# Expert weights in halves: 8 KB tiles for gate and up, and a new place for each weight transfer's issue

## The chip, the core and the metric

The kernel runs on one core of a Trainium2 chip. The metric is the device time of one execution in microseconds. The core has five engines that run side by side: PE (TensorE, matrix products), ACT (ScalarE), DVE (VectorE), POOL (GpSimd) and SP (SyncE, which here only issues DMA transfers). Sixteen DMA engines move data between HBM and the on-chip memory.

## What is computed

Two layers of a decoder over 1024 tokens of width 1024, all in float32. Each layer is a mixer (two groups of eight attention heads) followed by a mixture of experts, with a final norm behind the second layer. The change lies in the experts. Each token picks one of 8 groups and 2 of the 4 experts in it; each of the 32 experts has three matrices:

```python
def expert_block(args):
    xb, e = args
    h = jax.nn.silu(xb @ w_gate[e]) * (xb @ w_up[e])   # w_gate, w_up: 1024 x 256
    return h @ w_down[e]                               # w_down: 256 x 1024
...
contrib = ybuf[dest].astype(jnp.float32) * g_sorted[:, None]
y = jax.ops.segment_sum(contrib, tok_sorted, num_segments=T)
```

## The kernel before

A float32 product is made of three passes on TensorE (`mm3`, L190): each operand is split into a rounded part "hi" and a remainder "lo", and hi x hi, hi x lo and lo x hi are added up. So every weight that arrives must first be cast: ACT writes hi (L1464), DVE writes lo (L1465).

One layer runs as mixer, output projection with routing (loop at L1245), then the experts. The experts' loop (L1556) has 33 turns. In turn n TensorE makes the gate and up products of expert n in two halves (`gate_up`, 8 chunks of 128 rows of the weights), the transposes of expert n+1's tokens (`turn_x`) and the down products of expert n-1 (`down`, 2 chunks). Each expert has one block of 96 token rows, gathered by POOL three turns ahead; POOL also scatters the results.

The casts go in pieces of 128 x 1024 numbers, six for an expert: pieces 0 to 3 are its gate and up weights (two chunks of both matrices each), pieces 4 and 5 its down weights. `ORDER` (L52) fixes their sequence: in turn n come (n,4), (n,5), (n+1,0), (n+1,1), (n+1,2), (n+1,3). Seven pairs of hi and lo tiles (NHL, L46) go round among them.

The order of work on PE, ACT, DVE and POOL is written out by hand (`manual_schedule`, L96). SP is not in that list: a planner places its transfers, with the order in which they are written as their priority, and waits for a tile's room to be free.

Raw weights arrive as follows. Gate and up of one expert share one tile of 16 KB a partition (`gu_tile`, L333): two transfers of 1 MB (`load_gu`, L336), each partition reading 8 rows of 256 numbers, 8 KB in one run. The pool "mix" (L842) holds four such tiles; in the mixer the same four hold `mixT`, the transposed mixer output (hi and lo). Expert 0 has a tile of its own (L1234). Experts 1 to 3 are loaded in the routing loop (L1293), expert 4 when the experts' stage is opened (L1526), and expert n+5 by `load_a`, written at the head of turn n (L1558); its room is that of expert n+1. The down weights have four tiles of 8 KB a partition (`load_dn`, L330: one transfer of 1 MB, 8 KB runs); `load_b` of expert e+4 is written behind piece (e,5) (L1548). In the last layer tiles of the same pool take the residual for the final norm (L1583).

The hidden values of an expert (`hs`) are transposed in two parts (`flip_h`, L1493), with the column order that the layout of the down weights asks for.

Of the kernel before, what the change touches and what calls it, by code (L numbers as in the profile page):

```python
# [9 lines left out]
F32 = mybir.dt.float32  # L10
# [10 lines left out]
P = 128  # L21
# [60 lines left out]
def kernel(ctx: ExitStack, tc: tile.TileContext, x, positions, attn_norm, w_in, b_f, q_norm, w_uq,  # L82
# [245 lines left out]
        return [gain_flip] + [w[0][0], w[1][0], w[0][1], w[2][0], w[1][1], w[3][0], w[2][1], w[3][1]]  # L328

    def load_dn(raw, wd_, eng):  # L330
        eng.dma_start(raw, wd_.rearrange("(p k) n -> p k n", k=2))

    def gu_tile(p, tag="mix"):  # L333
        return p.tile([P, 2, KC, FF], F32, name="gu", tag=tag)

    def load_gu(raw, wg_, wu_):  # L336

        for g, w_ in enumerate((wg_, wu_)):
            sp.dma_start(raw[:, g], w_.rearrange("(p k) n -> p k n", k=KC))

    def wa_load(raws, l, k):
        raw = raws.tile([P, 512], F32, name="raw")[:, :MISC]
# [23 lines left out]
    def mixer(l, opened):  # L366
# [472 lines left out]
        pp_close()  # L839


        mp, mp_close = open_pool(f"mix{l}", "right", 4)  # L842
        mixT = [mp.tile([P, 2, KC, 2 * P], F32R, name="mix") for _ in range(4)]
        wor, wor_close = open_pool(f"wor{l}", "right", 2)
        att, att_close = open_pool(f"att{l}", "left", 3)
        tps, tps_close = open_pool(f"tps{l}", bufs=2, space=PSUM)
# [101 lines left out]
        def fin_c(p, half, bank=1):  # L948
            ysb = pairs[p][0].rearrange("p t s d -> p t (s d)")

            pt = ybank[bank].rearrange("p (t n) -> p t n", n=P)
            for i in range(4):
                pe.transpose(pt[:, i], ysb[:, half * 4 + i], ident)
            g = gain("fox" if p < 4 else "mla", l, p % 4)
            ms = [([mixT[2 * half + q][:, s] for s in range(2)], pt[:, 2 * q:2 * q + 2].rearrange("p a b -> p (a b)")) for q in range(2)]
            for m, src in ms:
                act.activation(m[0][:, p], src, AF.Copy, scale=g)
            for m, src in ms:
                dve.scalar_tensor_tensor(m[1][:, p], src, g, m[0][:, p].bitcast(F32), op0=OP.mult, op1=OP.subtract)
# [27 lines left out]
        ht_ = {}  # L987

        def out_mm(i, c, ks):
            m, ts, cs = [mixT[i // 2][:, s] for s in range(2)], slice(i % 2 * P, (i % 2 + 1) * P), slice(c * 512, c * 512 + 512)  # L990
            if ks[0] == 0:
                ht_[i, c] = ybank[0] if (i, c) == (1, 1) else op_.tile([P, 512], F32, name="ps")
            mm3(ht_[i, c], lambda k: m[0][:, k, ts], lambda k: m[1][:, k, ts],
                lambda k: w_at(k, 0, cs), lambda k: w_at(k, 1, cs), ks, first=ks[0] == 0, last=ks[-1] == KC - 1)
# [108 lines left out]

        def halves(j):
            hi, lo = hl[j]
            raw = early[0][:, :, 2 * j:2 * j + 2].rearrange("p g k n -> p g (k n)")
            hi, lo = (w.rearrange("p (g n) -> p g n", g=2) for w in (hi, lo))
            act.activation(hi, raw, AF.Copy)
            pool.tensor_tensor(lo, raw, hi.bitcast(F32), op=OP.subtract)
# [121 lines left out]

        hts = {i: resid(i) for i in range(2)}

        early = [v1.tile([P, 2, KC, FF], F32, name="V", tag="V")]  # L1234
        load_gu(early[0], w_gate[l, 0], w_up[l, 0])
        groups, going, state = {4: (0, 4), 6: (4, 6)}, deque(), [None]

        def route_on(n, pe_=False):
# [6 lines left out]
        for i in range(NT):  # L1245
            if i + 2 < NT:
                hts[i + 2] = resid(i + 2)
            if i > 1:
                out_mm(i, 0, range(4))
                if i < 4:  # L1250
                    route_b(i - 2)
                if i > 2:
                    route_a(i - 1, 0)
                    route_a(i - 1, 1)
                out_mm(i, 0, range(4, KC))
            add(i, 0)
            if i == NT - 1:
                norm_half(0)
            route_on(ROA)
            if i:  # L1260
                out_mm(i, 1, range(4))
                route_on(1, True)
                if i > 2:
                    route_b(i - 1)
                else:
                    route_a(i - 1, 0)
                    route_a(i - 1, 1)
                if i == NT - 1:
                    route_a(i, 0)
                out_mm(i, 1, range(4, KC))  # L1270
            if i == NT - 1:

                ops_close()
                vr2_close()
                hp, hl_close = open_pool(f"hl{l}")
                hl = slots(hp, 4)
                halves(0)
            add(i, 1)
            if i in groups:
                going.append(route_group(fs, *groups[i]))  # L1280
            if i < NT - 1:
                route_on(ROB)
                norm(i)
            else:
                route_a(i, 1)
                route_on(ROB)
                norm_half(1)
                route_b(i)
                halves(1)
                norm(i)  # L1290
                halves(2)
                halves(3)
            if i % 2 and i < NT - 1:  # L1293
                early.append(gu_tile(mp))
                load_gu(early[-1], w_gate[l, len(early) - 1], w_up[l, len(early) - 1])
            if i in DNAT:
                j = DNAT.index(i)
                load_dn(downs[j], w_down[l, j], sp)
# [102 lines left out]
    def slots(p, n):  # L1401
        return [[p.tile([P, D], F32R, name=f"{w}{i}") for w in ("hi", "lo")] for i in range(n)]

    def moe_open(l, v0, v1, mp, early, downs, dn_close, hl, hl_close, spare_close):
        scatters, parts = [], {}

        def pools_for(n, deep):
            rw, c1 = open_pool(f"er{n}{l}", "right")
            if deep:
                downs.extend(rw.tile([P, 2, D], F32, name=f"dn{j}") for j in range(2, NDN))  # L1410
            hp, c2 = open_pool(f"eh{n}{l}", "right")
            pools = {"rw": rw, "hl": deque(hl + slots(hp, NHL - 4) if deep else slots(hp, 6)), "gu": (mp, "mix") if deep else (rw, "gu0")}

            def more():
                pools["xs"], c3 = open_pool(f"ex{n}{l}", "left", 2 if deep else 1)
                pools["pp"], c4 = open_pool(f"ep{n}{l}", bufs=2, space=PSUM)
                pools["close"] = lambda: (c4(), c3(), c2(), c1(), (dn_close(), hl_close()) if deep else None)

            return pools, more

        def expert(pools, wg_, wu_, wd_, gi, si, n=None):
# [4 lines left out]
            ps_ = lambda *a, **k: pools["pp"].tile(*a, **k)  # L1426
            par = 0 if n is None else n % 2

            def load_a():
                if n is not None and n < len(early):  # L1430
                    raw = early[n]
                else:
                    raw = gu_tile(*gp)
                    load_gu(raw, wg_, wu_)
                e["raw"] = [raw[:, :, 2 * j:2 * j + 2].rearrange("p g k n -> p g (k n)") for j in range(4)]

            def parts_of(pairs):
                for hi, lo in pairs:
# [54 lines left out]
            def flip_h():  # L1493
                pt = ps_([P, 4, RB], F32, name="ph", bufs=1)
                for c in range(2):
                    pe.transpose(pt[:, c], e["hs"].rearrange("r (p k) -> r k p", k=2)[:, c], ident[0:RB, 0:RB])
                e["hT"] = [parts["xt"][:, 2 * par + s, KC * RB:(KC + 2) * RB].rearrange("p (k r) -> p k r", r=RB) for s in range(2)]
                split(e["hT"][0], e["hT"][1], pt[:, 0:2])

# [38 lines left out]
    def moe(l, m):  # L1538
# [5 lines left out]
        def pieces_to(n):  # L1544
            while pieces and n_pieces - len(pieces) < n:
                e, j = pieces.popleft()
                E[e]["piece"](j, pool if j in ONPOOL else dve)
                if j == 5 and e + NDN < NE:  # L1548
                    E[e + NDN]["load_b"]()

        pieces_to(PC0)
        E[0]["turn_x"]()
# [2 lines left out]
        kept = []  # L1555
        for n in range(NE + 1):  # L1556
            cur, prev, nxt = (E[k] if 0 <= k < NE else None for k in (n, n - 1, n + 1))
            if n + 5 < NE:  # L1558
                E[n + 5]["load_a"]()
            if n + NXB < NE:  # L1560
                E[n + NXB]["gather"]()
            if cur:
                cur["gate_up"](0)
            pieces_to(6 * n + PC[0])
            if prev:
                prev["flip_h"]()
            if cur:
                cur["gate_up"](1)
            if nxt:
                nxt["turn_x"]()  # L1570
            if prev:
                prev["down"]()
            pieces_to(6 * n + PC[1])
            if cur:
                cur["silu"]()
            if nxt:
                nxt["split_x"]()
            pieces_to(6 * n + PC[2])
            if prev:
                prev["result"]()  # L1580
            if l == DEPTH - 1 and n >= KEPT and len(kept) < NT:

                raw = gu_tile(mp).rearrange("p g k n -> p (g k n)")  # L1583
                for t in range(4):
                    kept.append(raw[:, t * D:(t + 1) * D])
                    sp.dma_start(kept[-1], h_d[2 * l][len(kept) - 1])
            pieces_to(6 * n + 6)
        pools["close"]()
        if l < DEPTH - 1:
# [101 lines left out]
```

## Time and profile before

| | us |
|---|---|
| median of 3 runs | 1969.77 (1967.16 to 1974.84) |
| the profiled execution, device time | 1971.02 |
| its span, first to last instruction | 1969.2 |
| TensorE busy | 1753.9 (89%) |
| VectorE busy | 1360.1 (69%) |
| ScalarE busy | 1178.5 (60%) |
| GpSimd busy | 651.4 (33%) |

The durations come from the one profiled execution. An engine's busy share is an average over the mixer, the routing and the experts, which have different limits, so the stages are looked at one by one. In the slices of the page each digit stands for 49 us; a 9 means 90% or more. In a timeline row the first number is the start, the second the duration (of all instructions merged into the row, "x3"), and the bracket tells how long the engine sat idle before it and what ended that. "SPq" rows are issues: the time is that of issuing, not of moving the data.

### The profile page before, as it was taken

Reading aid. Unit: us, or ns where it says so; the run is one execution under the profiler, and the core shown is the slowest. Engines: PE = TensorE matmul, PEld = TensorE weight load, DVE = VectorE, ACT = ScalarE, POOL = GpSimd, SP = SyncE. Lnnn points to the kernel's source line nnn. Section 1 sums busy time; section 2 is a strip of 40 time slices with the busy share of each in tenths; the row PEclk is TensorE's granted clock in tenths of the full one; section 3 lists DMA queues with packets and bytes.
Section 4 is the critical chain, followed back from the end, with each engine's and each line's share of the span. In section 5 each row is a group of like instructions: output and inputs, shape, how many; then the busy total and the mean of one; then the engine's idle time right before and its main releaser. Section 6 shows DMA issues by size and latency. Waiting matters only on the chain. (4 is left out here: it accounts for less than half of the span.)

```text
span 1969.2 us, 33380 instructions
## 1 busy us (share of the span) xinstructions
PE 1753.9 (89%) x12509; PEld 1414.7 (72%) x12509; DVE 1360.1 (69%) x2172; ACT 1178.5 (60%) x2254; POOL 651.4 (33%) x857
## 2 busy tenths in 40 slices
PE   7999799999994999999499997999999769999970
PEld 6987688888883776666399876888878647766640
DVE  6464389887346898888665345888853679987865
ACT  4443378888213888777344235888851258877751
POOL 4001154234105334554330021623341333345525
PEclk9999999999996999999799998999999979999985
DMA  4247832453754899998841775344446469999966
GB/s 159 65 120 219 269 125 102 107 128 80 276 176 147 314 364 373 363 363 292 289 147 52 205 232 201 122 109 109 109 172 227 171 218 359 366 368 357 362 238 219
DMA packets 118753, 427.07 MB, mean 217 GB/s; under 512 B 20118, under 2 KB 35516, under 8 KB 90940
## 3 DMA queue, kind: packets, MB, share of 16 engines
q1 hardware_dynamic: 103676, 387.13, 58.7%
q0 software_dynamic: 14336, 33.58, 5.1%
q10 hardware_dynamic: 576, 4.19, 0.7%
q8 instruction: 100, 1.64, 0.4%
q14 instruction: 65, 0.53, 0.1%
HBM read 347.24 MB, written 94.37 MB: 224 GB/s over the span
## 5 line engine op out<-in xcount | busy, mean ns | idle before, releaser
L1465 DVE TENSOR_TENSOR lo<-gu,hi 128x1024 fp32r<-128x1024 f32 x248 | 294.0, 1218 | 12.3 <-ACT hi L1464 11.5
L1464 ACT ACTIVATE hi<-gu 128x1024 fp32r<-128x1024 f32 x248 | 255.4, 1059 | 0.0
L1514 POOL DMA_INDIRECT y<-V,sidx x64 | 139.2, 2175 | 328.8 <-ACT V L1513 314.2
L873 PE MATMUL S<-op 96*128 96x512 f32 (+3 forms) x960 | 229.0, 372 | 19.5 <-DMA op<-FK 12.7
L885 DVE TENSOR_REDUCE nm<-S 128x1 f32<-128x1024 f32 (+7 forms) x256 | 183.2, 752 | 68.9 <-PE S L877 68.8
L894 ACT ACTIVATE pr<-S,nm 128x1024 f32<-128x1024 f32 (+7 forms) x256 | 189.2, 755 | 37.6 <-DVE nm L885 37.5
L195 PE MATMUL gu<-lo,V 128*96 128x512 f32 x512 | 205.2, 401 | 6.9 <-DVE lo L1465 6.7
L194 PE MATMUL gu<-hi,V 128*96 128x512 f32 x512 | 206.9, 404 | 0.5 <-ACT V L184 0.5
L196 PE MATMUL gu<-hi,V 128*96 128x512 f32 x512 | 205.6, 402 | 1.0
L1465 DVE TENSOR_TENSOR lo<-dn,hi 128x1024 fp32r<-128x1024 f32 x128 | 156.4, 1223 | 62.6 <-ACT hi L1464 59.1
L904 ACT ACTIVATE ph<-pt 128x512 f16<-128x512 f32 x288 | 157.3, 601 | 66.9 <-PE pt L902 65.9
L905 DVE SCALAR_TENSOR_TENSOR pl<-pt,ph 128x512 f16<-128x512 f32 x288 | 184.7, 683 | 8.7 <-ACT ph L904 7.8
L873 PEld LDWEIGHTS S<-op 96*128 96x128 f32 (+1 forms) x960 | 161.5, 196 | 36.9 <-DMA wor<-in_w_o_dram 14.9
L1464 ACT ACTIVATE hi<-dn 128x1024 fp32r<-128x1024 f32 x128 | 135.0, 1056 | 75.4 <-DMA dn<-in_w_down_dram 75.4
L902 PE MATMUL pt<-ident,pr 128*128 128x128 f32 x1152 | 154.9, 278 | 8.6 <-DVE pl L905 3.6
L902 PEld LDWEIGHTS pt<-ident,pr 128*128 128x128 f32 x1152 | 125.2, 143 | 14.0 <-ACT pr L894 13.2
L916 PE MATMUL y<-V,ph 128*128 128x64 f16 x2304 | 121.6, 193 | 2.8 <-ACT ph L904 1.6
L195 PEld LDWEIGHTS gu<-lo,V 128*96 128x96 f32 x512 | 83.5, 163 | 52.4 <-DVE lo L1465 22.7
L916 PEld LDWEIGHTS <-ph 128*128 128x128 f16 x2304 | 116.9, 98 | 5.2 <-ACT ph L904 1.8
L916 PE MATMUL y<-V,pl 128*128 128x64 f16 x1152 | 117.0, 193 | 1.1 <-DVE pl L905 1.0
L196 PEld LDWEIGHTS gu<-hi,V 128*96 128x96 f32 x512 | 83.1, 162 | 46.2 <-DVE V L185 14.8
L175 POOL TENSOR_SCALAR rs_v<-ss 128x1 f32<-128x1 f32 (+1 forms) x44 | 20.3, 461 | 289.3 <-ACT xn L1096 151.0
(363 smaller groups left out, 4393.7 us busy)
## 6 DMA issues: line engine op xcount, KB each, us to landing
gu<-in_w_gate_dram SPq DMA_DIRECT2D x62, 1024.0 KB
gu<-in_w_up_dram SPq DMA_DIRECT2D x62, 1024.0 KB
dn<-in_w_down_dram SPq DMA_DIRECT2D x60, 1024.0 KB
raw<-in_w_in_dram SPq DMA_DIRECT2D x48, 256.0 KB
h<-ht SPq DMA_DIRECT2D x17, 512.0 KB
FQ<-st SPq DMA_DIRECT2D x32, 256.0 KB
FK<-st SPq DMA_DIRECT2D x32, 256.0 KB
MQ<-st SPq DMA_DIRECT2D x16, 512.0 KB
```

The source lines that it names most:

```text
L194: pe.matmul(ps, sh(kc), mh(kc), start=first and i == 0, stop=False)
L195: pe.matmul(ps, sh(kc), ml(kc), start=False, stop=False)
L196: pe.matmul(ps, sl(kc), mh(kc), start=False, stop=last and i == n - 1)
L873: pe.matmul(o, a[0:k, qs], b[0:k, c0:c0 + n], start=bank not in started, stop=pi == len(passes) - 1 and not diag, skip_group_check=True)
L885: dve.tensor_reduce(nm, u["S"][:, col:col + (qb + 1) * P], axis=AX.X, op=OP.max, negate=True)
L894: act.activation(u["pr"][:, s], u["S"][:, s], AF.Exp, bias=nm, accum_out=zst[h // 2][:, qb, h % 2:h % 2 + 1])
L902: pe.transpose(pt[:, b], u["pr"][:, (4 * q + b) * P:(4 * q + b + 1) * P], ident)
L904: act.activation(u["ph"][:, ks], pt, AF.Copy, scale=P_SCALE)
L905: dve.scalar_tensor_tensor(u["pl"][:, ks], pt, P_SCALE, u["ph"][:, ks], op0=OP.mult, op1=OP.subtract)
L916: pe.matmul(yst[h][:, qb], a[:, b], v[:, kb, h % H, c], start=first_y[h], stop=(kb == qb and s == 2), skip_group_check=True)
L1464: act.activation(h_, raw, AF.Copy)
L1465: eng.tensor_tensor(l_, raw, h_.bitcast(F32), op=OP.subtract)
```

## The change

Gate and up of an expert are loaded in two halves. A half (`gu_half`) is a tile of 8 KB a partition that holds four of the eight rows of both matrices in every partition: two transfers of 512 KB, in runs of 4 KB. The pool "mix" has eight tiles of this size instead of four of twice the size, and `mixT` takes them as separate tiles for hi and lo. Expert 0's own tile is laid out by halves as well, with four transfers.

The transfers of experts 5 to 31 are written elsewhere: the first half of expert e+4 behind piece (e,1), the second behind piece (e,3), where `load_b` already stands behind piece (e,5). The line at the head of the turn is gone.

The down weights are laid out with chunk c holding rows 128c to 128c+127 (before: every second row), so that a partition reads two runs of 4 KB; `flip_h` takes contiguous columns accordingly. The tiles of the last residual loads are halved in size. Only what follows from the layouts is left out below.

```diff
     def load_dn(raw, wd_, eng):
-        eng.dma_start(raw, wd_.rearrange("(p k) n -> p k n", k=2))
-
-    def gu_tile(p, tag="mix"):
-        return p.tile([P, 2, KC, FF], F32, name="gu", tag=tag)
-
-    def load_gu(raw, wg_, wu_):
-
+        eng.dma_start(raw, wd_.rearrange("(k p) n -> p k n", p=P))
+
+    def gu_half(p, wg_, wu_, q, tag="mix"):
+
+        raw = p.tile([P, 2, KC // 2, FF], F32, name="gu", tag=tag)
+        ks = slice(q * 4, q * 4 + 4)
         for g, w_ in enumerate((wg_, wu_)):
-            sp.dma_start(raw[:, g], w_.rearrange("(p k) n -> p k n", k=KC))
+            sp.dma_start(raw[:, g], w_.rearrange("(p k) n -> p k n", k=KC)[:, ks])
+        return raw
...
-        mp, mp_close = open_pool(f"mix{l}", "right", 4)
-        mixT = [mp.tile([P, 2, KC, 2 * P], F32R, name="mix") for _ in range(4)]
+        mp, mp_close = open_pool(f"mix{l}", "right", 8)
+        mixT = [[mp.tile([P, KC, 2 * P], F32R, name="mix") for _ in range(2)] for _ in range(4)]
...
-        early = [v1.tile([P, 2, KC, FF], F32, name="V", tag="V")]
-        load_gu(early[0], w_gate[l, 0], w_up[l, 0])
+        raw0 = v1.tile([P, 2, 2, 4, FF], F32, name="V", tag="V")
+        early = [[raw0[:, 0], raw0[:, 1]]]
+        for q in range(2):
+            for g, w_ in enumerate((w_gate, w_up)):
+                sp.dma_start(raw0[:, q, g], w_[l, 0].rearrange("(p k) n -> p k n", k=KC)[:, q * 4:q * 4 + 4])
...
             if i % 2 and i < NT - 1:
-                early.append(gu_tile(mp))
-                load_gu(early[-1], w_gate[l, len(early) - 1], w_up[l, len(early) - 1])
+                early.append([gu_half(mp, w_gate[l, len(early)], w_up[l, len(early)], q) for q in range(2)])
...
-            def load_a():
+            def load_a(*qs):
                 if n is not None and n < len(early):
-                    raw = early[n]
+                    raw = e["halves"] = early[n]
                 else:
-                    raw = gu_tile(*gp)
-                    load_gu(raw, wg_, wu_)
-                e["raw"] = [raw[:, :, 2 * j:2 * j + 2].rearrange("p g k n -> p g (k n)") for j in range(4)]
+                    raw = e.setdefault("halves", [])
+                    for q in qs or range(2):
+                        raw.append(gu_half(gp[0], wg_, wu_, q, gp[1][q]))
+                if len(raw) < 2:
+                    return
+                e["raw"] = [raw[q][:, :, k:k + 2].rearrange("p g k n -> p g (k n)") for q in range(2) for k in (0, 2)]
...
-                    pe.transpose(pt[:, c], e["hs"].rearrange("r (p k) -> r k p", k=2)[:, c], ident[0:RB, 0:RB])
+                    pe.transpose(pt[:, c], e["hs"][:, c * P:(c + 1) * P], ident[0:RB, 0:RB])
...
                 if j == 5 and e + NDN < NE:
                     E[e + NDN]["load_b"]()
+                if j in (1, 3) and 0 < e < NE - 4:
+                    E[e + 4]["load_a"](j // 2)
...
-            if n + 5 < NE:
-                E[n + 5]["load_a"]()
...
-                raw = gu_tile(mp).rearrange("p g k n -> p (g k n)")
-                for t in range(4):
-                    kept.append(raw[:, t * D:(t + 1) * D])
-                    sp.dma_start(kept[-1], h_d[2 * l][len(kept) - 1])
+                for raw in [mp.tile([P, 2, 4, FF], F32, name="gu", tag="mix") for _ in range(2)]:
+                    for t in range(2):
+                        kept.append(raw[:, t].rearrange("p k n -> p (k n)"))
+                        sp.dma_start(kept[-1], h_d[2 * l][len(kept) - 1])
```

## Rows read from the trace of the kernel before

**Rows 1.** The page: busy us, share and instructions; DMA share in 40 slices.

```profile
PE 1753.9 (89%) x12509; PEld 1414.7 (72%) x12509; DVE 1360.1 (69%) x2172; ACT 1178.5 (60%) x2254; POOL 651.4 (33%) x857
...
DMA  4247832453754899998841775344446469999966
```

**Rows 2.** Windows of layer 0's experts: length, busy by engine, clock, DMA share, GB/s.

```profile
660.00:757.00 97.00, 97.00 (x488) 70.60 (x487) 91.09 (x107) 86.39 (x128) 36.60 (x31) 1.00 1.01 365
757.00:905.00 148.00, 143.24 (x680) 95.83 (x679) 121.99 (x145) 116.28 (x176) 77.40 (x45) 1.00 0.98 364
914.00:930.00 16.00, 15.09 (x68) 9.89 (x69) 14.62 (x20) 13.84 (x22) 4.02 (x2) 1.00 0.54 210
```

**Rows 3.** Timeline of ACT, casts of layer 0: start, us, instruction, idle before.

```profile
758.66 1.06 ACT L1464 ACTIVATE hi<-dn 128x1024 fp32r<-128x1024 f32 x1 [1.23 <-DMA dn<-in_w_down_dram]
...
860.59 1.06 ACT L1464 ACTIVATE hi<-dn 128x1024 fp32r<-128x1024 f32 x1 [2.42 <-DMA dn<-in_w_down_dram]
...
930.91 1.06 ACT L1464 ACTIVATE hi<-dn 128x1024 fp32r<-128x1024 f32 x1 [1.27 <-DMA dn<-in_w_down_dram]
...
934.99 2.01 ACT L1464 ACTIVATE hi<-gu 128x1024 fp32r<-128x1024 f32 x2
...
938.79 1.07 ACT L1464 ACTIVATE hi<-dn 128x1024 fp32r<-128x1024 f32 x1
```

**Rows 4.** Waits (us in total, times, longest), 820 to 880, then 900 to 960.

```profile
ACT hi L1464 <- DMA dn<-in_w_down_dram: 12.1, 6, 2.6
...
ACT wah L184 <- DMA y<-V,sidx: 5.4, 1, 5.4
```

**Rows 5.** Timeline of SP, weight transfers issued in layer 0.

```profile
639.60 0.34 SPq L331 DMA_DIRECT2D dn<-in_w_down_dram  x1
649.11 0.33 SPq L339 DMA_DIRECT2D gu<-in_w_gate_dram  x1
...
694.35 0.33 SPq L339 DMA_DIRECT2D gu<-in_w_gate_dram  x1
...
695.20 0.42 SPq L331 DMA_DIRECT2D dn<-in_w_down_dram  x1
...
749.53 0.33 SPq L339 DMA_DIRECT2D gu<-in_w_gate_dram  x1
...
832.81 0.33 SPq L331 DMA_DIRECT2D dn<-in_w_down_dram  x1
...
860.58 0.33 SPq L339 DMA_DIRECT2D gu<-in_w_up_dram  x1
```

**Rows 6.** Waits of SP itself, 640 to 940: us in total, times, longest.

```profile
SPq L339 <- DVE lo L1465: 145.2, 27, 9.1
...
SPq L331 <- DMA gu<-in_w_gate_dram: 31.2, 16, 2.5
```

**Rows 7.** Timeline of DVE: expert 1's casts 1 to 3, layer 0, then layer 1.

```profile
645.58 3.50 DVE L1465 TENSOR_TENSOR lo<-gu,hi 128x1024 fp32r<-128x1024 f32 x3 [0.31 <-ACT hi L1464]
...
1602.00 3.50 DVE L1465 TENSOR_TENSOR lo<-gu,hi 128x1024 fp32r<-128x1024 f32 x3 [0.31 <-ACT hi L1464]
```

**Rows 8.** Windows of layer 1's stream and of the final stage, columns as above.

```profile
1608.00:1613.00 5.00, 5.00 (x26) 3.56 (x24) 4.95 (x8) 5.00 (x9) 0.95 (x1) 1.00 1.02 421
1916.00:1921.00 5.00, 0.00 (x0) 0.00 (x0) 3.07 (x3) 0.46 (x1) 0.00 (x0) 0.50 1.03 415
1925.00:1950.00 25.00, 0.00 (x0) 0.00 (x0) 19.30 (x16) 5.10 (x9) 16.57 (x30) 0.50 0.84 288
```

**Rows 9.** Timeline of SP, the final stage's first loads, 512 KB each.

```profile
1912.52 3.72 SPq L224 DMA_DIRECT2D y<-y  x7
```

**Rows 10.** Waits of SP itself, whole span: stores of the norm.

```profile
SPq L1102 <- DVE xn L1098: 89.0, 14, 10.7
```

**Rows 11.** Weight loads of L1496 and L1472: ns min/median/max, first and last start.

```profile
L1496 PEld LDWEIGHTS ph<-ident,hs x128: 194/196/201, 647.9 to 1902.8; 96*128 96x128 f32 x128
...
L1472 PEld LDWEIGHTS pt<-ident,x x160: 138/140/143, 650.9 to 1871.2; 96*128 96x128 f32 x160
```

More of the change, by code (lines that the diff above doesn't have):

```diff
@@ L954, in fin_c @@
             g = gain("fox" if p < 4 else "mla", l, p % 4)
-            ms = [([mixT[2 * half + q][:, s] for s in range(2)], pt[:, 2 * q:2 * q + 2].rearrange("p a b -> p (a b)")) for q in range(2)]
+            ms = [(mixT[2 * half + q], pt[:, 2 * q:2 * q + 2].rearrange("p a b -> p (a b)")) for q in range(2)]
             for m, src in ms:
@@ L989, in out_mm @@
         def out_mm(i, c, ks):
-            m, ts, cs = [mixT[i // 2][:, s] for s in range(2)], slice(i % 2 * P, (i % 2 + 1) * P), slice(c * 512, c * 512 + 512)
+            m, ts, cs = mixT[i // 2], slice(i % 2 * P, (i % 2 + 1) * P), slice(c * 512, c * 512 + 512)
             if ks[0] == 0:
@@ L1105, in halves @@
             hi, lo = hl[j]
-            raw = early[0][:, :, 2 * j:2 * j + 2].rearrange("p g k n -> p g (k n)")
+            raw = early[0][j // 2][:, :, j % 2 * 2:j % 2 * 2 + 2].rearrange("p g k n -> p g (k n)")
             hi, lo = (w.rearrange("p (g n) -> p g n", g=2) for w in (hi, lo))
@@ L1411, in pools_for @@
             hp, c2 = open_pool(f"eh{n}{l}", "right")
-            pools = {"rw": rw, "hl": deque(hl + slots(hp, NHL - 4) if deep else slots(hp, 6)), "gu": (mp, "mix") if deep else (rw, "gu0")}
+            pools = {"rw": rw, "hl": deque(hl + slots(hp, NHL - 4) if deep else slots(hp, 6)), "gu": (mp, ("mix", "mix")) if deep else (rw, ("gu0", "gu1"))}
             def more():
```

## Prediction

> **What bounds the kernel now.** I read the page's busy shares and its slices first [rows 1]: TensorE is busy 89% of the span, which looks like the bound, but the DMA digits stand at 9 in two stretches, slices 13 to 18 and 32 to 37. Those are the expert stages of the two layers, the only places that the change reaches. The windows of layer 0's stage come next [rows 2]: TensorE is busy 97.0 of 97 us up to 757 and 143.2 of 148 us after it, while the DMA share is 1.01 and 0.98 throughout. So the stage begins as a matmul loop and ends as a DMA stream. What ends last is read from the casts [rows 3]. I call (e,4) the first cast of expert e's down weights and (e,0) to (e,3) those of its gate and up weights; iteration n of the loop at L1556 casts (n,4), (n,5), (n+1,0) to (n+1,3). From 758.66, iteration 13 by count, the first down cast waits for its own transfer in every iteration (12.1 us in six of them [rows 4]), so the pace is that of the stream: 930.91 - 758.66 = 172.25 us for 17 iterations, 10.13 us each. Before it the pace is TensorE's: gate transfers go out at 694.35 and 749.53, six iterations later [rows 5], 9.20 us each. At that pace iteration 30 would start near 758.66 + 17 x 9.20 = 915, and it starts at 930.91: the stream costs at least 16 us a layer. This is the most that any reordering of it can win.
>
> An expert's weights are 3 MB, so the stream lands 1 MB in 10.13 / 3 = 3.38 us. The queue is not emptied by SyncE: in the late part a down transfer waits to be issued until an older gate transfer is done (16 times [rows 6]). The down transfer issued at 832.81 ends ACT's wait at 860.59, and the up transfer eight places later in the queue goes out at 860.58 [rows 3, 5]. I read that as eight transfers in flight.
>
> **Part by part.**
>
> *An earlier start.* SyncE's first gate transfer of the stage goes out only when expert 1's last cast is done: its casts (1,1) to (1,3) end at 645.58 + 3.50 = 649.08 and the transfer starts at 649.11 [rows 5, 7]. Between the one down transfer at 639.60 and 649.11 nothing is issued. With halves, the room of (1,0) and (1,1) is free at 645.58 + 3.50 / 3 = 646.75. A half pair is 1 MB, 3.38 us, and the second half is free at 649.08, so the stream runs on without a hole. Gain 2.3 us; layer 1 has the same three casts, 1602.00 and 3.50 us [rows 7], so 2.3 us again.
>
> *The order.* Before, load_a(n+5) is written at the head of iteration n and load_b(n+4) after cast (n,5). The late queue is gate, up, then down (694.35, 695.20 [rows 5]): the down weights that an iteration casts first stand behind 2 MB that it casts later. After, the order written is down, first half, second half, which is the order of the casts. Take the end of layer 0. dn(30) lands at 930.91 and dn(31) 1 MB behind it. After, the same places of the stream are held by the second half of expert 31 (930.91) and by dn(31) (934.3); dn(30) lands 2 MB, 6.8 us, earlier. Cast (31,2) is the second of the pair at 934.99, so it starts at 935.9 [rows 3]; it could start at 930.9, 5.0 us earlier. The cast of dn(31) starts at 938.79; it could start at 934.3, 4.5 us earlier. The smaller one decides: 4.5 us a layer. What is late next is dn(31), then the second half. All that follows (matmuls, scatter, the next stage, which waits for the last scatter [rows 4]) moves with it. The same edit takes away a blockage: a down transfer that is free waits on SyncE behind a gate transfer whose cast is not done. In the changed order each wait is later than the one ahead of it, so no free transfer stands behind a wait.
>
> *Lines of 4 KB.* Gate and up were read in runs of 8 KB a partition, down as well; after, all are runs of 4 KB and gate and up come in transfers of 512 KB. Both kinds are in the trace, each with the queue full [rows 8]: from 1608 to 1613, at the head of layer 1's stream, 8 KB runs move 421 GB/s; from 1916 to 1921 the final stage's seven transfers of 512 KB with 4 KB runs [rows 9] move 415. That is 1.4% slower. The weights from the first gate to dn(30) are 80 MB = 83.9e6 bytes, at 365 GB/s [rows 2] 230 us; 1.4% is 3.3 us a layer. The other end is the stretch 1925 to 1950, 4 KB reads mixed with writes: 288 GB/s at share 0.84, 343 at full share, against 364 / 0.98 = 371 in the expert stage, 7.6% or 17.5 us a layer. The writes there are many more than the expert stage's scatter, so I take the value of the reads. No row shows 4 KB runs ahead of 8 KB ones, so zero is the other end.
>
> *Fewer bytes in flight.* Eight transfers were 8 MB; with four of 512 KB and one of 1 MB per expert they are 5 MB, 17 us of stream. SyncE's longest wait for a cast is 9.1 us [rows 6], so the queue does not run dry, and a loss is excluded on this count. There may be a gain. The first 29 MB of the stream (gu(5) to dn(13)) took 758.66 - 649.11 = 109.6 us, 3.78 us each, at the same 365 GB/s as the later ones at 3.38. The bytes moved but did not complete a transfer: some of the 16 engines ran ahead of the slowest. The end shows it too: from 914 to 930 the share is 0.54 and 210 GB/s [rows 2], though dn(30) is still not there. That lead costs 29 x (3.78 - 3.38) = 11.6 us. If it shrinks as the bytes in flight, 3/8 of it, 4.4 us, come back. Between 0 and 4.4 I take 2.0: the 0.54 row shows that a lead exists, so not zero; the 11.6 also holds the time in which the first transfer starts up, so not the whole.
>
> *What costs nothing.* SyncE issues five transfers instead of three, 0.33 us each [rows 5], 1.7 us in 10.13: hidden. In the routing stage four experts' gate and up loads and expert 4's are ten more issues, 3.3 us a layer, ahead of which residual loads and stores queue; SyncE sleeps there until the norm is done (89.0 us in 14 waits [rows 10]), so I take 0 and keep 3.3 as a bound. The transposes of hs read contiguous columns: weight loads of 196 ns become 140 [rows 11], 0.11 us an expert, under the stream's cover until the last two or three, 0.3 us at most. The split mixT and the halved tiles of the last residual loads change no instruction.
>
> *Sum.* 2.3 + 4.5 + 2.0 - 3.3 = 5.5 us a layer, 11.0 in all. The profiled execution took 1971.0 us (span 1969.2): 1960.0. It lies 1.2 us above the median of the three runs, 1969.8, so the forecast against the median is 1959.
>
> **Rivals.** *The order is not kept.* SyncE is not among the engines whose order is written by hand, and the trace shows the planner at work: the first down transfer goes out ahead of the gate transfer written before it [rows 5]. If the halves again go ahead of the down weights, the 4.5 us are lost: 1968. For it: that row. Against it: the late queue follows the written order, and the written order is now that of the releases. *Half price.* 4 KB runs cost 4% in the mix with gathers and scatters, 9.2 us instead of 3.3: 5.5 - 5.9 = -0.4 a layer, 1971. *The slower side: the stream is slower than its bytes.* Its place is every transfer from expert 5 on, its price the mixed stretch's 7.6%, 17.5 us: 17.5 - 3.3 = 14.2 us a layer worse, 1959 + 28 = 1987. It passes 0.5% slower (9.8 us in all) when the runs cost 5.5 + 4.9 + 3.3 = 13.7 us a layer, 6%. Against it: the seven 512 KB transfers at 415 GB/s, which have the very shape. The Trainium skill, page "DMA: Bandwidth & Descriptors", section "Rules for kernel authors", speaks for this rival: most bandwidth wants 128 partitions and at least 1 MiB per DMA, and the change goes below it. The 415 GB/s of 512 KB transfers disagree with that where several are queued. *More.* The lines cost nothing and the lead gives its 4.4: 2.3 + 4.5 + 4.4 = 11.2 a layer, 1947.
>
> **How the numbers follow.** About 0.5% (9.8 us) is what a measurement of this kernel can tell from no change, so faster is below 1960 and slower above 1980. The forecast case, 1952 to 1967 by its own terms, has 0.55, of which 0.33 lies below 1960. "More" has 0.16, the lost order 0.10, half price 0.07, the slower side 0.12. So faster 0.49, same 0.39, slower 0.12. The range 1947 to 1975 leaves out the slower side and a little of "more".
>
> **What would show it.** Right: in each expert stage the first gate half goes out some 2.3 us earlier, behind the second gate and up cast of expert 1; SyncE's order is down, two first halves, two second halves; ACT's waits for DMA are split between down and gate/up; the pace late in the stage is 10.2 to 10.3 us; the cast of dn(30) starts near 925 and that of dn(31) near 933 in layer 0. Wrong: a pace of 10.6 us or more (the lines cost more than 1.4%), down transfers behind gate and up (order lost), or stretches of the stage with a DMA share well under 1 (the queue runs dry).

## The result

Five runs of each kernel give medians of 1958.54 us after (1957.11 to 1960.09) and 1967.16 us before (1966.57 to 1974.84): 8.6 us apart. The ratio on record for these runs is 0.9938, interval 0.9924 to 0.9953, which is 12 us of 1970 (9 to 15). The two readings differ by 3.6 us, and the five runs of before spread over 8 us, so the gain is some 9 to 12 us. The profiled execution of after took 1960.09 us (span 1958.3), 10.9 us below that of before. The forecast was 1959 us, 11 us less than before. Differences between kernels below are taken from the ratios unless two medians are named.

The page of after, busy shares and DMA digits in the slices, against [rows 1]:

```profile
PE 1745.1 (89%) x12509; PEld 1410.6 (72%) x12509; DVE 1366.3 (70%) x2172; ACT 1185.7 (61%) x2254; POOL 588.1 (30%) x857
...
DMA  5247833453764999999841775344446569999975
```

The engines execute the same instructions. GpSimd's 63 us less are its scatters, whose records shorten from 2175 to 1127 ns each; all kernels below with the new order have 1101 to 1240 ns and all others 2020 to 2212. Why is open, and GpSimd, 30% busy, does not set the time. What matters is how the expert stage fills its time. SyncE's first weight transfers in layer 0 of after, against [rows 5]:

```profile
640.55 0.39 SPq L331 DMA_DIRECT2D dn<-in_w_down_dram  x1
646.83 0.33 SPq L338 DMA_DIRECT2D gu<-in_w_gate_dram  x1
647.22 0.42 SPq L338 DMA_DIRECT2D gu<-in_w_up_dram  x1
649.10 0.33 SPq L338 DMA_DIRECT2D gu<-in_w_gate_dram  x1
649.48 0.42 SPq L338 DMA_DIRECT2D gu<-in_w_up_dram  x1
651.64 0.38 SPq L331 DMA_DIRECT2D dn<-in_w_down_dram  x1
```

The first half goes out at 646.83, and 649.11 was the start before. The order is down, first half, second half. ACT's casts of after, the first that waits for a down transfer, then dn(30) and dn(31), the first down casts of the last two experts, against [rows 3]; below them the waits of ACT for DMA between 820 and 880, against [rows 4]:

```profile
794.29 1.06 ACT L1469 ACTIVATE hi<-dn 128x1024 fp32r<-128x1024 f32 x1 [0.76 <-DMA dn<-in_w_down_dram]
...
925.98 1.06 ACT L1469 ACTIVATE hi<-dn 128x1024 fp32r<-128x1024 f32 x1 [0.76 <-DMA dn<-in_w_down_dram]
...
934.97 1.05 ACT L1469 ACTIVATE hi<-dn 128x1024 fp32r<-128x1024 f32 x1
...
ACT hi L1469 <- DMA dn<-in_w_down_dram: 3.5, 4, 1.3
ACT hi L1469 <- DMA gu<-in_w_up_dram: 3.1, 4, 1.3
```

The stage keeps TensorE's pace for longer: the first late cast is at 794.29, iteration 17, where it was 758.66, iteration 13. From there the pace is (925.98 - 794.29) / 13 = 10.13 us, that of the stream. Waiting for down weights alone, 12.1 us in six iterations, has become 3.5 + 3.1 us shared between down and up. The row that marks the head of layer 0's stage, expert 1's three casts on DVE, stands at 645.58 in both traces, so the casts compare directly: dn(30) at 930.91 before and 925.98 after, dn(31) at 938.79 and 934.97. Layer 1, the same casts of after, and dn(31) of before:

```profile
1593.52 3.50 DVE L1470 TENSOR_TENSOR lo<-gu,hi 128x1024 fp32r<-128x1024 f32 x3 [0.30 <-ACT hi L1469]
...
1884.64 1.05 ACT L1469 ACTIVATE hi<-dn 128x1024 fp32r<-128x1024 f32 x1
```

```profile
1895.88 1.06 ACT L1464 ACTIVATE hi<-dn 128x1024 fp32r<-128x1024 f32 x1
```

That is 291.1 us from expert 1's casts to dn(31); before it was 1602.00 [rows 7] to 1895.88, 293.9 us. So 3.8 + 2.8 = 6.6 of the 10.9 us lie between those two casts. Another part lies ahead of them. Waits of TensorE for the first expert's gathered tokens, in layers 0 and 1, before:

```profile
PE pt L1472 <- DMA V<-xn,gidx: 11.4, 1, 11.4
...
PE pt L1472 <- DMA V<-xn,gidx: 10.4, 1, 10.4
```

and after:

```profile
PE pt L1477 <- DMA V<-xn,gidx: 10.2, 1, 10.2
...
PE pt L1477 <- DMA V<-xn,gidx: 9.2, 1, 9.2
```

1.2 us less in each layer, 2.4 in all: a gain that the prediction has no term for. The remaining 1.9 us lie behind dn(31) and in the mixer. Last, the windows 660 to 757, 757 to 905 and 905 to 930 of after, against [rows 2] (columns as there; the last two are DMA share and GB/s):

```profile
660.00:757.00 97.00, 97.00 (x491) 69.97 (x490) 91.09 (x108) 86.96 (x129) 37.17 (x31) 1.00 1.02 358
757.00:905.00 148.00, 143.98 (x700) 98.55 (x699) 129.00 (x151) 122.94 (x180) 52.20 (x46) 1.00 1.00 356
905.00:930.00 25.00, 23.34 (x114) 15.44 (x113) 21.14 (x25) 19.95 (x30) 4.70 (x5) 1.00 0.96 354
```

Two things stand here. The stream carries 358 and 356 GB/s at full share where it carried 365 and 364: something in the change costs rate. And it now runs on to the end of the stage at 0.96. The last of the three windows in before:

```profile
905.00:930.00 25.00, 23.85 (x110) 15.45 (x109) 21.35 (x27) 20.15 (x30) 8.95 (x5) 1.00 0.70 267
```

There the share had fallen to 0.70 while the casts still waited for dn(30).

### The profile page after: what moved, and what is told of

Read it like the earlier page. It is cut to its first block, busy times and chain, and to the rows that moved or that the text cites. A ratio compares the mean times of both kernels' runs of the same rounds, so it can differ in the third digit from the quotient of the medians.

```text
span 1958.3 us, 33744 instructions
## 1 busy us (share of the span) xinstructions
PE 1745.1 (89%) x12509; PEld 1410.6 (72%) x12509; DVE 1366.3 (70%) x2172; ACT 1185.7 (61%) x2254; POOL 588.1 (30%) x857
## 4 chain that ended last, share of the span: by engine, by line
PE 28%; DMA 14%; DVE 4%; ACT 3%; issue 2%; POOL 1%; SPq 0%; POOLq 0%; ACTq 0%; DVEq 0%
DMA gu<-in_w_gate_dram 5%; PE ps L194 5%; PE ps L195 5%; PE ps L196 5%; DMA gu<-in_w_up_dram 4%; PE S L873 4%; PE pt L902 3%; DMA dn<-in_w_down_dram 2%; PE y L916 2%; ACT pr L894 1%; DVE nm L885 1%; PE gu L195 1%; PE gu L196 1%; PE gu L194 1%; DMA y<-y 1%
## 5 line engine op out<-in xcount | busy, mean ns | idle before, releaser
L1470 DVE TENSOR_TENSOR lo<-gu,hi 128x1024 fp32r<-128x1024 f32 x248 | 298.6, 1221 | 44.8 <-ACT hi L1469 43.4
L1519 POOL DMA_INDIRECT y<-V,sidx x64 | 72.1, 1127 | 385.9 <-ACT V L1518 369.4
L873 PEld LDWEIGHTS S<-op 96*128 96x128 f32 (+1 forms) x960 | 161.5, 196 | 36.5 <-DMA wor<-in_w_o_dram 13.6
```

Of the source, the lines that this page charges most:

```text
L873: pe.matmul(o, a[0:k, qs], b[0:k, c0:c0 + n], start=bank not in started, stop=pi == len(passes) - 1 and not diag, skip_group_check=True)
L1470: eng.tensor_tensor(l_, raw, h_.bitcast(F32), op=OP.subtract)
```

## The experiments

A ratio is to the kernel before, run on the same chip, with its interval; 1 per mille is 1.97 us. The name in brackets is the one that the expectations use.

**Runs of 4 KB alone.** (`lines_1mb`) Whole transfers of 1 MB and the order of before, but all weights in runs of 4 KB. The down weights' edit is that of the change and not shown again.

```diff
-        return p.tile([P, 2, KC, FF], F32, name="gu", tag=tag)
+        return p.tile([P, 2, 2, KC // 2, FF], F32, name="gu", tag=tag)
...
-            sp.dma_start(raw[:, g], w_.rearrange("(p k) n -> p k n", k=KC))
+            sp.dma_start(raw[:, :, g], w_.rearrange("(p q k) n -> p q k n", q=2, k=KC // 2))
```

> The kernel before, with its two 1 MB transfers for gate and up and its 1 MB for down, but all read in runs of 4 KB (the raw tile is laid out by halves, down as in the change). Room, order and bytes in flight are those of before, so this measures the 4 KB runs alone. My sum: 3.3 us a layer slower, 6.6 us in all over the kernel before. If runs of 4 KB cost nothing: 0. If they cost the 7.6% of the mixed stretch: 28 to 35 us slower.

Measured 0.9978 (0.9969 to 0.9987), median 1967.07 against 1970.7: 4.3 us faster by the ratio, where a loss was expected. The stream's rate is that of before, 367 and 363 GB/s:

```profile
660.00:757.00 97.00, 97.00 (x487) 69.83 (x486) 90.07 (x105) 86.05 (x128) 39.32 (x33) 1.00 1.02 367
757.00:905.00 148.00, 143.48 (x679) 94.13 (x678) 124.10 (x149) 117.58 (x177) 79.30 (x43) 1.00 0.99 363
```

The wait for the first gathered tokens is 10.3 and 9.3 us, as in after, which is 2.2 of the 4.3 us. So runs of 4 KB throughout cost the stream nothing that these windows show, and the opening gains. Where the other 2 us come from is not shown.

**The same with halved transfers.** (`lines_half`) Gate and up come in four transfers of 512 KB into the whole tile; nothing else differs from the run above.

```diff
-        for g, w_ in enumerate((wg_, wu_)):
-            sp.dma_start(raw[:, :, g], w_.rearrange("(p q k) n -> p q k n", q=2, k=KC // 2))
+        for q in range(2):
+            for g, w_ in enumerate((wg_, wu_)):
+                sp.dma_start(raw[:, q, g], w_.rearrange("(p q k) n -> p q k n", q=2, k=KC // 2)[:, q])
```

> As lines_1mb, but gate and up in four transfers of 512 KB into the same whole tile, so eight transfers hold 5 MB instead of 8. Room and order as before. My sum: the lead of the faster engines shrinks, 2.0 us a layer better than lines_1mb, so 2.6 us over the kernel before in all. If the bytes in flight don't matter: the time of lines_1mb. If small transfers cost by themselves: slower than lines_1mb.

Measured 1.0001 (0.9989 to 1.0012), 4.5 us slower than with whole transfers. The rate falls while the DMA share stays full:

```profile
660.00:757.00 97.00, 97.00 (x488) 69.79 (x487) 89.10 (x103) 85.27 (x125) 39.22 (x33) 1.00 1.01 362
757.00:905.00 148.00, 143.02 (x671) 92.51 (x670) 122.47 (x148) 116.50 (x177) 80.23 (x42) 1.00 1.00 357
```

5 and 6 GB/s less, 1.4 to 1.7%. Layer 1 agrees: 355 and 354 GB/s from 1616 to 1710 and from 1710 to 1860, against 360 and 361 with whole transfers. The loss that the prediction expected of the runs comes with the halving of the transfers.

**The order undone.** (`order_undone`) After, with both halves of expert n+5 written at the head of turn n again.

```diff
-                if j in (1, 3) and 0 < e < NE - 4:
-                    E[e + 4]["load_a"](j // 2)
...
+            if n + 5 < NE:
+                E[n + 5]["load_a"]()
```

> The changed kernel, halves and 4 KB runs and all, with both halves of expert n+5 written at the head of turn n again, ahead of the down transfer. My sum: the 4.5 us a layer of the order are lost and the rest stays, 1.0 us a layer or 2.0 us in all faster than the kernel before. If the finer room is what helps: 8 to 9 us faster than before, like the changed kernel.

Measured 0.9964 (0.9953 to 0.9975), median 1964.12, 2.6 per mille or 5 us above after, though the two intervals touch. Between 820 and 880 ACT waits for down weights alone again:

```profile
ACT hi L1469 <- DMA dn<-in_w_down_dram: 13.0, 6, 2.4
```

**The order alone.** (`order_alone`) Before, with whole gate and up tiles and 8 KB runs, but issued behind the cast that frees the tile.

```diff
+                if j == 3 and 0 < e < NE - 4:
+                    E[e + 4]["load_a"]()
...
-            if n + 5 < NE:
-                E[n + 5]["load_a"]()
```

> The kernel before, whole tiles and 8 KB runs, with the transfer of expert e+4 written behind the cast (e,3) instead of the head of the turn: the order of the change alone. My sum: 4.5 us a layer, 9.0 us in all faster than before. If the halves are needed: no change.

Measured 0.9991 (0.9979 to 1.0003): 1.8 us, not 9, and zero lies inside the interval. The wait has changed its name and kept its size. Waits of ACT between 820 and 880, and a late cast of gate and up, (30,0):

```profile
ACT hi L1464 <- DMA gu<-in_w_up_dram: 12.6, 6, 2.4
...
923.56 1.06 ACT L1464 ACTIVATE hi<-gu 128x1024 fp32r<-128x1024 f32 x1 [2.11 <-DMA gu<-in_w_up_dram]
```

12.1 us on down weights have become 12.6 us on up weights. A cast of gate and up takes rows of both matrices, so (n+1,0) needs the last byte of both 1 MB transfers; the down weights are early and nothing is won. My expectation was wrong by the prediction's own arithmetic, whose 4.5 us rest on the first half landing as a unit.

**The order with whole transfers in 4 KB runs.** (`whole_1mb_order`) The first experiment's kernel with the edit above.

> The kernel before with 4 KB runs in transfers of 1 MB (as lines_1mb) and the order of the change, on whole tiles: against half_in_one only the room differs, against lines_1mb only the order. Revised theory: order and room remedy the same thing, a free down transfer that stands behind a gate transfer whose room is not free, so with the order in place room is worth little (half_order equalled the changed kernel): 4 to 6 us a run slower than half_in_one at most, 15 to 21 us faster than before. If the order gives only what it gave alone on 8 KB runs (2 us): 6 us faster than before. If room is worth its 2.3 us a layer of earlier start by itself: 16 us faster than before.

Measured 0.9971 (0.9959 to 0.9982): 0.7 per mille on top of 0.9978, inside the intervals. ACT waits 14.6 us in seven turns for up weights. Of the expectation's cases the one with 6 us came: the length of the runs is not what the order lacked. Its "only the room differs" against `half_in_one`, further below, overlooks that there a half also lands by itself; the next experiment keeps the two apart.

**The order with halved transfers, rooms whole.** (`half_order`) The second experiment's kernel with the same edit: each half lands by itself, but the room is that of the whole tile, so a transfer can't start earlier than before.

> Whole tiles of 16 KB as before, so room comes free only behind the cast (e,3), but four transfers of 512 KB, 4 KB runs and the order of the change. It differs from the changed kernel in nothing but when room is free. Revised theory, since lines_half was no faster than before and order_undone 7 us faster than that: the room is worth 3.5 us a layer, and the order only some 2 without it, because expert 31's first half can't land ahead of its second by much less than 2 MB; so 2 to 5 us faster than before. If the order gives the same with or without the room (2.6 per mille, the ratio of the changed kernel to order_undone): 5 us faster. If room is worth nothing: 12 us faster, like the changed kernel.

Measured 0.994 (0.9927 to 0.9953), median 1959.9: 12 us below the same kernel without the order (1.0001), and level with after. Its first gate transfer and the ones behind it, SyncE's timeline, then ACT's waits for DMA between 820 and 880:

```profile
644.80 0.34 SPq L340 DMA_DIRECT2D gu<-in_w_gate_dram  x1
645.19 0.42 SPq L340 DMA_DIRECT2D gu<-in_w_up_dram  x1
645.67 0.42 SPq L340 DMA_DIRECT2D gu<-in_w_gate_dram  x1
646.13 0.43 SPq L340 DMA_DIRECT2D gu<-in_w_up_dram  x1
...
ACT hi L1465 <- DMA gu<-in_w_up_dram: 5.9, 6, 2.0
ACT hi L1465 <- DMA dn<-in_w_down_dram: 4.0, 5, 1.5
```

The four transfers go out together, when the whole tile is free (expert 1's casts end at 644.78 in this trace), and the time is that of after all the same. With the order in place the earlier start is worth nothing that these runs can tell. Without the order it is worth something: the order undone (0.9964) has the finer rooms and lies 3.7 per mille below the second experiment (1.0001), which has not.

**Down weights in 8 KB runs, the rest as after.** (`down_8k`)

```diff
-        eng.dma_start(raw, wd_.rearrange("(k p) n -> p k n", p=P))
+        eng.dma_start(raw, wd_.rearrange("(p k) n -> p k n", k=2))
```

> The changed kernel with the down weights in runs of 8 KB again (and the transposes of hs by every second column). Revised theory: runs of 4 KB cost nothing in the stream, but the gathers at the head of the stage, which share the DMA engines with two down transfers, are 1 to 2 us quicker beside 4 KB runs; so this is 2 to 4 us slower than the changed kernel, 8 to 10 us faster than before. My old sum (4 KB runs cost 1.4%, down is a third of the bytes): 2.2 us faster than the changed kernel, 14 us faster than before.

Measured 0.9962 (0.9948 to 0.9975): 2.4 per mille or 4.7 us slower than after by intervals that just overlap, and by medians of one chip 6.1 us slower than the run before it here (1966.04 against 1959.9), which is level with after. The first wait for gathered tokens is 11.1 and 10.4 us, that of before, and the rate between 757 and 905 is 349 GB/s where after has 356 (348 against 353 from 1710 to 1860). These rows come from an execution of 1972.17 us, 6 us above the median of its kernel. So the layout of the down weights seems to carry part of the gain, in the opening and in the stream; how much, these runs tell only roughly.

**Down weights in 4 KB runs, the rest as before.** (`down_4k`) The opposite edit on the kernel before.

> The kernel before with the down weights alone in runs of 4 KB; gate and up stay at 8 KB in 1 MB transfers. Revised theory: most of what lines_1mb gained (4.3 us) is in the opening, where the gathers run beside down transfers, so 2 to 4 us faster than before. If the gain comes from the runs of gate and up: 0 to 1.5 us faster. My old sum: 2.2 us slower.

Measured 1.0019 (1.001 to 1.0029), 3.7 us slower. The opening does gain (10.1 and 9.1 us), but between 757 and 905 the stream carries 357 GB/s where before carried 364. In layer 1 it carries 355 against 361 from 1616 to 1710 and 361, as before, from 1710 to 1860. These two kernels mix runs of 8 and 4 KB in one queue, and in layer 0 each carries 7 GB/s less than the kernel of one length that it was made from. Whether the mixture is the cause, and why it should cost, is open.

**One transfer of 1 MB for a half.** (`half_in_one`) After, with the gate and up weights handed over stacked in one array, so that a half of both is one transfer of 1 MB in 4 KB runs: three transfers an expert instead of five.

```diff
-        for g, w_ in enumerate((wg_, wu_)):
-            sp.dma_start(raw[:, g], w_.rearrange("(p k) n -> p k n", k=KC)[:, ks])
+        sp.dma_start(raw.rearrange("p g k n -> p g (k n)"), w_.rearrange("g (p q k) n -> p q g (k n)", q=2, k=KC // 2)[:, q])
```

> The changed kernel, but with gate and up laid side by side in one array in HBM, so that a half is one transfer of 1 MB in the same 4 KB runs instead of two of 512 KB. Three transfers an expert, 8 MB in flight. Revised theory: lines_half lost 4.5 us against lines_1mb by halving the transfers and the bytes in flight; that comes back, 4 to 5 us faster than the changed kernel, 16 to 17 us faster than before. My old sum: 2.0 us a layer slower than the changed kernel, because the faster engines run further ahead; 8 us faster than before.

Measured 0.9895 (0.9881 to 0.9909), median 1950.6: 4.3 per mille or 8.5 us below after, faster than both kernels of the case, with the same rooms, order and runs. The windows:

```profile
660.00:757.00 97.00, 97.00 (x486) 69.82 (x485) 91.07 (x106) 86.86 (x128) 38.60 (x33) 1.00 1.02 367
757.00:905.00 148.00, 144.18 (x711) 100.42 (x710) 129.96 (x153) 123.81 (x182) 53.19 (x46) 1.00 0.99 358
```

In the first 97 us the rate is back at 367, against 358 in after, so the casts fall behind later (first late down cast at 819.74, iteration 20, against 794.29), and TensorE starts 711 matmuls in the second window against 700. In that window the rate is 358, only 2 GB/s above after; layer 1 has the same pattern (366 and 357 against 355 and 353), so the rate comes back in the first part of a stage and hardly in the second. This and the second experiment agree on the sign of what halving costs, with 8.5 and 4.5 us. The Trainium skill, page "DMA: Bandwidth & Descriptors", section "Rules for kernel authors", asks for at least 1 MiB a transfer; the prediction set that aside on one row, and these two runs bear the rule out. Whether the bytes in flight or a price per transfer is behind it no run here separates.

**Two down transfers out of the gathers' way.** (`down_later_before`) When the experts' stage opens, ACT issues the down transfers of experts 2 and 3 beside the first gathers on POOL. In before, from its timeline:

```profile
624.85 1.26 POOL L1456 DMA_INDIRECT V<-xn,gidx  x1 [6.55 <-DVE gd L1218]
...
625.36 0.39 ACTq L331 DMA_DIRECT2D dn<-in_w_down_dram  x1
...
625.77 0.45 ACTq L331 DMA_DIRECT2D dn<-in_w_down_dram  x1
```

Here, in the kernel before, they are issued behind expert 0's token split.

```diff
-        for e in range(2, NDN):
-            m["E"][e]["load_b"](act)
...
+        for e in range(2, NDN):
+            E[e]["load_b"](act)
```

> The kernel before, 8 KB runs, with one edit: the two down transfers of experts 2 and 3, which ACT issues while the first gathers run, are issued by ACT behind the split of the first gathered tokens. Theory: they hold up the gathers by 8 KB packets, and 4 KB runs help only because they hold them up less; so without them the first turn starts 2 to 4 us earlier in layer 0 and about 1 us earlier in layer 1, 3 to 5 us faster than before in all, the gain of lines_1mb or more. If the gathers are not held up: no change, or slower by the time that those down weights come later.

Measured 0.9953 (0.994 to 0.9967), median 1963.04 against 1971.58: 9 us faster. The waits for the first gathered tokens, layers 0 and 1:

```profile
PE pt L1470 <- DMA V<-xn,gidx: 6.4, 1, 6.4
...
PE pt L1470 <- DMA V<-xn,gidx: 6.3, 1, 6.3
```

11.4 - 6.4 and 10.4 - 6.3 make 9.1 us, the whole gain. The gather is issued at 624.83, as before, and the down transfers now at 630.94, so what changed is how soon the gather lands. The opening of the stage waits for a gather that shares the DMA engines with 2 MB that nobody needs yet.

**Both together.** (`half_in_one_later`) Stacked halves and the later down transfers.

> half_in_one with the same edit. Theory: beside 4 KB runs the gathers are still held up, by less; 1 to 3 us faster than half_in_one, 22 to 24 us faster than before. If 4 KB runs have taken all of it: the time of half_in_one.

Measured 0.9889 (0.9871 to 0.9908), median 1948.39, the fastest kernel seen. The waits fall to 6.7 and 6.4 us as they should, but the total moves by only 0.6 per mille, inside the intervals: in this kernel the stream sets the end of the stages, and an earlier first matmul does not bring it forward by as much. From expert 1's casts to dn(31), both layers together, the trace has 578.1 us where that of stacked halves alone has 574.3: 3.8 of the 6.4 us that the two waits give are lost again, and the first late cast is that of iteration 17 (786.8) and not 20. That rests on one trace of each kernel.

## Why the prediction came out right, step by step

The time was right to 1 us, and the gain of 11 us lies between the two readings of the measured one. But two of the four terms of the sum had the wrong sign, and a third, the start, gave nothing on top of the order; that the total came out all the same is luck. (A small misreading on the way: the DMA digits of [rows 1] are 9 in four and five slices, 14 to 17 and 33 to 37 counted from 0, and not in all of 13 to 18 and 32 to 37.)

- *What bounds the stage*: right. After ends layer 0 at the same 10.13 us an expert as before [rows 3], where 10.2 to 10.3 was forecast, and the gains in the stage came with changes of the transfers alone, the work of the engines unchanged.
- *An earlier start*, 2.3 us a layer, and *the order*, 4.5: 13.6 us in all. The second experiment and after differ in exactly these two: 1.0001 to 0.9938, 6.3 per mille or 12.4 us. The sum holds; its split does not. The start came at the predicted moment, 646.83 for 646.75, but it added nothing to the order. Four kernels with halved transfers in 4 KB runs have the two edits in all combinations; the last column is the time from expert 1's casts to dn(31), both layers added up, one trace each:

| kernel | ratio | casts to dn(31), us |
|---|---|---|
| neither (`lines_half`) | 1.0001 | 592.8 |
| half tiles as rooms (`order_undone`) | 0.9964 | 585.8 |
| order (`half_order`) | 0.9940 | 581.6 |
| both (after) | 0.9938 | 580.5 |

  The finer rooms, half tiles that come free by themselves, give 7 us alone and the order 12; on top of the rooms the order gives 5, and on top of the order the rooms give nothing that can be told. Adding the two was the mistake: they overlap. Why is not shown. In before SyncE waits for DVE's casts 145.2 us with gate and up transfers [rows 6], and in after, over the same 640 to 940:

```profile
SPq L338 <- DMA dn<-in_w_down_dram: 69.9, 22, 4.6
SPq L338 <- DMA gu<-in_w_gate_dram: 49.4, 41, 4.0
SPq L338 <- DVE lo L1470: 37.1, 23, 5.8
```

  the casts hold these transfers for 37.1 us, and most of the rest is older transfers. But that is not the overlap: the kernel with neither edit is already down to

```profile
SPq L340 <- DVE lo L1466: 47.8, 9, 8.2
```

  so most of this fall comes with the halved transfers. The times forecast for the last casts are close: dn(30) near 925, found at 925.98, and dn(31) near 933, found at 934.97. "A half lands as a unit" was a condition of that term, not said as one; without it the order is worth 1 to 2 us, not clear of zero.
- *Lines of 4 KB*, -3.3 us a layer: wrong. The step that failed is the one that read 421 against 415 GB/s [rows 8] as a price of the run length. Those are two windows of 5 us, one in a queue just being refilled, the other with nothing else running; sustained, whole transfers in 4 KB runs move 367 and 363 GB/s, 8 KB runs 365 and 364. In time the runs gain 4.3 us, about half of it in the opening, where the trace of before shows the gather and the two down transfers side by side and no term of the sum looked; from expert 1's casts to dn(31) the two kernels differ by 0.7 us (586.4 against 587.1).
- *Fewer bytes in flight*, +2.0 a layer: wrong in sign. The bytes in flight did fall as worked out: a down transfer of after goes out at 847.17, and the cast that takes it, counted from the last expert backwards, starts at 864.80 after a short wait for it, 17.6 us, where 17 were estimated, and the eighth transfer behind it goes out at that moment:

```profile
847.17 0.38 SPq L331 DMA_DIRECT2D dn<-in_w_down_dram  x1
...
864.80 1.06 ACT L1469 ACTIVATE hi<-dn 128x1024 fp32r<-128x1024 f32 x1 [0.35 <-DMA dn<-in_w_down_dram]
...
864.84 0.33 SPq L338 DMA_DIRECT2D gu<-in_w_gate_dram  x1
```

  But no time came back: the halved transfers cost 4.5 us (second experiment) to 8.5 us (stacked halves). The low share at the end of the stage, which the prediction took as the sign that some DMA engines lead others (no view here shows them one by one), did go, from 0.70 to 0.96 between 905 and 930; the halving alone has little part in that (0.73 with whole transfers in 4 KB runs, 0.78 with halved ones). The sentence that failed is "so the queue does not run dry, and a loss is excluded on this count". The share did stay at 1.00; the rate under it fell from 363 to 357. A full DMA share does not say that the engines move all they could.
- *What costs nothing*: right as far as it shows. The transposes' weight loads went from 196 to 141 ns (L1501), as said. No run isolates the ten more issues of the routing stage.

In total the prediction had 13.6 for start and order, -6.6 for lines and +4.0 for the lead. The runs give, in the order in which the kernels build on each other, 4.3 for lines, -4.5 for halves, 12.4 for start and order: 12.2 us in all, by the ratios.

Of the rivals, the lost order did not come: SyncE kept the written sequence. Its price, 9 us, was 5. The slower side priced the runs at 7.6% of the rate; the runs cost nothing, but its sentence on transfers below 1 MiB named a cost that is there, 1.4 to 1.7%.

## What to carry to other kernels

Where a stage runs at a stream's pace, ask of each transfer which cast or product needs it first and what it must hold to be of use alone: an order of issue pays only as finely as the data land. Two edits that end the same wait are not two terms of a sum; take the larger, and let a kernel with one of them decide. Look also at the first microseconds of the stage, where a small gather that all wait for may stand among megabytes that nobody needs yet.

## What the chip showed beyond that

*A gather beside plain loads.* The first gather of the experts' stage is waited for 11.4 us with two 1 MB loads in 8 KB runs beside it (10.8 to 11.4 over three kernels), 10.3 with the same loads in 4 KB runs (10.1 to 10.4 over eight), 6.4 without them. The Trainium skill, page "DMA: Bandwidth & Descriptors", section "Queues, rings and completion order", says that a DMA engine takes turns between queues a whole packet at a time; longer packets of another queue would then hold up a small transfer for longer. The three numbers agree in direction, and so do the packets that the pages of the profile count, in before and with all weights in 4 KB runs:

```profile
DMA packets 118753, 427.07 MB, mean 217 GB/s; under 512 B 20118, under 2 KB 35516, under 8 KB 90940
```

```profile
DMA packets 143329, 427.07 MB, mean 217 GB/s; under 512 B 20118, under 2 KB 35516, under 8 KB 140092
```

The total grows by 24576, and the packets of 8 KB or more fall by 24576: one for every run of 8 KB in the 192 weight transfers (128 partitions each). The turns between queues themselves no run here shows.

*An issue that waits.* A 1 MB transfer in 4 KB runs can keep SyncE in the issuing instruction for several microseconds. Issues of gate transfers, shortest, median and longest in ns, in the kernel before, with whole transfers in 4 KB runs, and (line L331) with stacked halves, each from the view of one line's instructions:

```profile
L339 SPq DMA_DIRECT2D gu<-in_w_gate_dram x62: 327/328/424, 522.8 to 1858.2; - x62
```

```profile
L339 SPq DMA_DIRECT2D gu<-in_w_gate_dram x62: 539/1790/5880, 522.5 to 1854.9; - x62
```

```profile
L331 SPq DMA_DIRECT2D gu<-in_w_gu_dram x124: 367/2768/5029, 524.2 to 1854.3; - x124
```

With 8 KB runs, or with gate and up in 512 KB transfers, the median issue takes 0.33 us, and SyncE waits on semaphores for older transfers ahead of it instead. So the prediction's reading of eight transfers in flight holds for the kernel before and for halved transfers, and for the two kernels with the long issues another limit comes first. Stacked halves are the faster for all that; SyncE only issues transfers.
